# One transformer pass with mixture of experts on one core: expert FFN steps of 2048 and 1536 columns in place of 1024, weight loads in runs of 8 and 6 KB, and 64 token slots without branches where weights stay whole

## The chip, the cores and the metric

The kernel runs on one NeuronCore of a Trainium2 chip. TensorE (PE) multiplies, VectorE (DVE) and ScalarE (ACT) work on elements, GpSimd (POOL) does small things and issues some loads, and SyncE (SP) issues nearly all DMAs, which 16 DMA engines carry out. The metric is the device time of one execution in microseconds (us); lower is better. About 0.2% (2.7 us) is what a measurement of this kernel can tell from no change.

## The reference

256 tokens of width 1024, all in fp32, go through two blocks. The first is a latent attention (MLA) with a dense SwiGLU FFN, the second a sparse attention (NSA) with a mixture of experts; a scaled residual and a layer norm follow each part. What this change touches is the last part alone:

```python
logits = (xt @ w_router)                      # 256 x 8
top_val, top_idx = lax.top_k(logits, 2)       # each token goes to 2 of 8 experts
wts = softmax(top_val)
# for every expert e and the tokens that chose it:
h = silu(xb @ w_gate[e]) * (xb @ w_up[e])     # 1024 -> 3584
y[tok] += (h @ w_down[e]) * weight            # 3584 -> 1024
```

The 256 tokens make 512 assignments, 64 per expert on average. The weights of the eight experts are 8 x 3 x 1024 x 3584 x 4 bytes = 352.3 MB, of 431 MB that the kernel moves in all.

## The kernel before

**Places.** The experts are worked through one after the other, in eight "places". Place 0 is expert 0; `arrange()` sorts the others by their token counts and puts the three with most tokens at places 1, 3 and 5. At the places of `PLAIN = 0, 2, 4, 6, 7` the weights are used as they come, as fp32 matrices; at 1, 3 and 5 every weight tile is first split on ACT (`act.copy`, line 120, to tile `whi`) and DVE (`tensor_tensor`, line 123, to `wlo`), and a product takes three fp32r matmuls: x-high by w-high, x-high by w-low, x-low by w-high. Only place 0's first 512 columns are done differently, for all tokens at once, while the routing is still being worked out.

**Steps.** A place is cut along the 3584 FFN columns into the steps of `widths(e)`: 1024, 1024, 1024 and 512 columns (place 0: 512 first). A step reads its gate chunks (`mg`), then its up chunks (`mu`), then the down chunks (`md`) of the step before it, in that order on PE, and the loads are planned in the same order by `moe_keys()`. A chunk is one tile of 128 partitions x 2048 floats, 1 MB. Of gate and up a partition gets two rows' pieces of 1024 columns (4 KB each), or in the step of 512 columns four pieces of 2 KB; of down it gets two rows of 4 KB.

**Buffers.** Each chunk has its place in SBUF long before it is needed: the lists `first` and `then` go round 13 tiles of 1 MB (five `raw`, then `s1`, `xTh`, `xTl`, `xna`, `s2`, `x3Tl`, the pair `whi`/`wlo` in two halves with a DMA each, and, once place 0 is through, `x3Th`). The first 18 chunks are fetched while the attention still runs. After that SP issues a chunk's DMA (line 94, line 81 for the pair) when the tile's last reader is done: the matmuls at a plain place, DVE's subtraction at a split one.

**Branches.** The number of token slots depends on a count that is known only at run time. So PE has both versions of each group of matmuls and jumps (`big_or_small`): at plain places `two()` for at most 64 tokens, which puts 64 slots twice on the array's 128 columns, each half with half of the weight columns, and `one()` for up to 128 slots; at split places `three()` or, for at most 64 tokens, `two()`. So that later instructions may read a whole PSUM bank in both cases, `two()` at plain places also fills unused banks with a zero product (`blank`: the matmuls of line 1689 that read `low`, into `pa` and `pt`), and ACT copies half a bank to `low` for `whole()`. Line 1689 is the helper `mm`, which issues every expert matmul; tiles tell them apart: `pa` is gate or up, `pb` is down, `raw` (or `whi`, `wlo` as buffers) the weights at plain places, `whi`/`wlo` with 128*128 the split ones.

**Around a place.** `gather` picks the tokens by one-hot matmuls (line 1493), `hid` (1510, 1511) does silu and product from PSUM, the hidden tile is transposed on PE (1538, 1560) and copied out (1518, 1519, 1565), `outs` and `scatter` (442, 443, 1844 to 1846) add the result to `y`. At the end `end()` works off the last down chunks, scatters and normalizes. A path for more than 128 tokens stands behind the end (`vmax > 128`).

Of the kernel before, what the change touches and what calls it, by code (L numbers as in the profile page):

```python
# [20 lines left out]
E = 8  # L21
# [5 lines left out]
def body(tc, a, out, tap=None, upto=9):  # L27
# [39 lines left out]
    def load(src, shape, where=None):  # L67
# [9 lines left out]
        if isinstance(where, list):  # L77
            rs = [w()[:, :h] for w in where]
            m = shape[0] // 2
            for i in range(2):  # L80
                sp.dma_start(rs[i].rearrange("p (a b) -> p a b", a=m), src[:, i * m:(i + 1) * m, :])
            return rs, n, shape
        r = where()
        v = r[:, :n]
        v = v.rearrange("p (a b) -> p a b", a=shape[0])
# [72 lines left out]
    for z in ("s1", "s2", "x3Th", "x3Tl"):  # L158
        places[z] = lambda z=z: slot(ep, z)()
# [206 lines left out]

    def moe_shape(key):
        c0, wd = widths(key[1])[key[2]]
        return (2, 1024) if key[0] == "md" and not key[4:] or key[0] != "md" and wd == 1024 else (4, 512)

    def moe_src(key):
        k, e, j, i = key[:4]
        c0, wd = widths(e)[j]
        w = a[{"mg": "moe_w_gate", "mu": "moe_w_up", "md": "moe_w_down"}[k]][0]
        w = w[0] if e == 0 else w[bass.ds(order[e], 1)][0]
        if k == "md":
            if key[4:]:
# [1679 lines left out]
```

## Time and profile before

| what | value |
|---|---|
| median of 3 runs | 1371.7 us (1371.13 to 1372.74) |
| the profiled execution's own time | 1371.53 us |
| its span, first to last instruction | 1369.8 us |
| moved | 430.95 MB, 168,529 packets |
| PE / DVE / ACT busy | 1309.6 / 741.7 / 632.0 us |
| granted TensorE clock, mean | 0.991 |

The profile is of one execution. 1.7 us of its time lie outside the span. PE's busy time is the union of overlapping matmuls whose ends are modelled, so a full row of nines on PE does not say that PE is the bound. A share of the DMA engines above 1 comes from packets that overlap on one engine.

### The profile page before, as it was taken

To read this page: it belongs to the slowest core of one execution; us is meant where nothing else is said; L and a number is where in the kernel's file an instruction comes from. 1 tells how busy PE (TensorE), PEld (TensorE's weight loads), DVE (VectorE), ACT (ScalarE), POOL (GpSimd) and SP (SyncE) were. 2 spreads that over 40 slices of the span, in tenths; PEclk is the share of its full clock that TensorE was granted. 3 is DMA by queue.
4 is the path that set the end of the run, shared out by engine and by line. 5 is a ranking of instruction groups with operands and counts; after the bars stand their busy time and mean duration, and the time that the engine had idled before them with its cause. 6 is when DMAs were issued, how large, how long until landed. Compare 5 with 4: busy or idle time off the path is not lost. (4 is left out here: it accounts for less than half of the span.)

```text
span 1369.8 us, 20185 instructions
## 1 busy us (share of the span) xinstructions
PE 1309.6 (96%) x7310; PEld 918.5 (67%) x7310; DVE 741.7 (54%) x1213; ACT 632.0 (46%) x989; POOL 42.8 (3%) x58
## 2 busy tenths in 40 slices
PE   8998999999999899999999999999999999998885
PEld 7878999989988683368874467884446886442331
DVE  5856545577678851268872158883227986200103
ACT  5554444446576540258771057882027885010001
POOL 0002000002000110000000000000000000000000
PEclk9999999999999999999999999999999999999998
DMA  9634555579522659999999999999999999999994
GB/s 312 208 119 156 184 186 185 185 206 253 170 82 67 230 206 356 409 408 408 402 407 408 402 409 408 403 407 405 407 403 408 409 400 389 409 402 409 409 402 158
DMA packets 168529, 430.95 MB, mean 315 GB/s; under 512 B 11935, under 2 KB 64421, under 8 KB 168400
## 3 DMA queue, kind: packets, MB, share of 16 engines
q1 hardware_dynamic: 165824, 421.00, 81.6%
q0 software_dynamic: 2576, 8.18, 2.0%
q8 instruction: 87, 1.43, 0.4%
q14 instruction: 42, 0.34, 0.1%
HBM read 428.08 MB, written 1.07 MB: 313 GB/s over the span
## 5 line engine op out<-in xcount | busy, mean ns | idle before, releaser
L123 DVE TENSOR_TENSOR wlo<-raw,whi 128x1024 fp32r<-128x1024 f32 (+1 forms) x341 | 404.6, 1215 | 186.8 <-ACT whi L120 176.7
L120 ACT CAST whi<-raw 128x1024 fp32r<-128x1024 f32 (+2 forms) x343 | 353.9, 1045 | 196.1 <-PE pa L1689 41.0
L1689 PE MATMUL pa<-raw,xe 128*64 128x512 f32 (+1 forms) x1128 | 233.2, 554 | 8.3 <-DMA raw<-in_moe_w_up_dram 4.4
L1689 PE MATMUL pa<-whi,xe 128*128 128x512 f32 (+2 forms) x716 | 229.8, 407 | 1.7 <-ACT whi L120 1.5
L1689 PEld LDWEIGHTS pa<-raw,xe 128*64 128x64 f32 x1128 | 77.8, 137 | 142.4 <-issue 107.6
L1689 PEld LDWEIGHTS pa<-whi,xe 128*128 128x128 f32 (+1 forms) x716 | 130.4, 186 | 40.4 <-issue 5.2
L1689 PE MATMUL pa<-wlo,xe 128*128 128x512 f32 (+2 forms) x380 | 142.8, 411 | 1.3 <-DVE wlo L123 1.2
L1689 PE MATMUL pb<-raw,four 128*64 128x512 f32 x528 | 130.5, 597 | 11.5 <-DMA raw<-in_moe_w_down_dram 8.4
L1565 ACT COPY four<-pt 128x512 f32<-128x512 f32 x19 | 11.1, 585 | 231.6 <-PE pt L1560 200.5
L1689 PE MATMUL pb<-whi,four 128*128 128x512 f32 (+1 forms) x352 | 115.1, 404 | 0.0
L1689 PEld LDWEIGHTS pb<-raw,four 128*64 128x64 f32 x528 | 39.0, 136 | 87.5 <-issue 71.4
L1511 DVE TENSOR_TENSOR four<-four,pa 128x512 f32<-128x512 f32 x57 | 36.9, 683 | 106.2 <-PE pa L1689 78.0
L1565 DVE COPY four<-pt 128x512 f32<-128x512 f32 x15 | 10.4, 691 | 152.7 <-PE pt L1689 152.7
L1689 PEld LDWEIGHTS pa<-wlo,xe 128*128 128x128 f32 (+1 forms) x380 | 66.7, 183 | 20.8 <-issue 3.1
L1689 PEld LDWEIGHTS pb<-whi,four 128*128 128x128 f32 (+1 forms) x352 | 65.3, 186 | 15.0
L1689 PE MATMUL pb<-wlo,four 128*128 128x512 f32 (+1 forms) x184 | 73.8, 412 | 0.0
L261 PE MATMUL pa<-xTh,whi 128*128 128x256 f32 x216 | 67.6, 313 | 0.0
L263 PE MATMUL pa<-xTh,wlo 128*128 128x256 f32 x216 | 61.1, 283 | 0.4 <-DVE wlo L123 0.4
L262 PE MATMUL pa<-xTl,whi 128*128 128x256 f32 x216 | 61.1, 283 | 0.0
L261 PE MATMUL pb<-xTh,whi 128*128 128x256 f32 x176 | 49.9, 284 | 0.0
L262 PE MATMUL pb<-xTl,whi 128*128 128x256 f32 x176 | 49.8, 283 | 0.0
L263 PE MATMUL pb<-xTh,wlo 128*128 128x256 f32 x176 | 49.8, 283 | 0.0
(423 smaller groups left out, 2075.5 us busy)
## 6 DMA issues: line engine op xcount, KB each, us to landing
raw<-in_moe_w_up_dram SPq DMA_DIRECT2D x105, 1024.0 KB, 16.5
raw<-in_moe_w_down_dram SPq DMA_DIRECT2D x102, 1024.0 KB, 16.4
raw<-in_moe_w_gate_dram SPq DMA_DIRECT2D x99, 1024.0 KB, 17.5
raw<-in_nsa_w_in_dram SPq DMA_DIRECT2D x23, 512.0 KB, 7.1
raw<-in_ffn_w_gate_dram SPq DMA_DIRECT2D x11, 1024.0 KB, 5.1
raw<-in_ffn_w_up_dram SPq DMA_DIRECT2D x11, 1024.0 KB, 5.1
raw<-in_ffn_w_down_dram SPq DMA_DIRECT2D x11, 1024.0 KB, 4.8
wlo<-in_moe_w_gate_dram SPq DMA_DIRECT2D x11, 512.0 KB, 15.7
```

The lines of the kernel that those rows point to most:

```text
L120: act.copy(hi[:, :h], src)
L123: (pool if later == "pool" else dve).tensor_tensor(lo[:, :h], src, f(hi[:, :h]), op=ALU.subtract)
L261: pe.matmul(o, lh, rh, start=first, stop=False)
L262: pe.matmul(o, lh, rl, start=False, stop=False)
L263: pe.matmul(o, ll, rh, start=False, stop=last)
L1511: dve.tensor_tensor(hh, sg, pu, op=ALU.mult)
L1565: eng(hT[:, i * 512:(i + 1) * 512], p)
L1689: pe.matmul(o, l, r, start=first, stop=last, skip_group_check=True)
```

## The change

1. **Wider steps, longer runs.** Steps are 2048 and 1536 columns (place 0: 512, 2048, 1024). A gate or up chunk of a wide step is 128 rows x the whole step: one run of 8 KB per partition (1 MB), or of 6 KB (768 KB). A down chunk gives a partition two neighbouring rows, one run of 8 KB, instead of rows p and p + 128; for this the hidden columns are taken odd and even (`hh[:, o:o + 255:2]`, `z[:, q::2]`) when they are transposed or multiplied. The last two down tails stay at 2 KB, and so does place 0's first step.
2. **64 slots, no branches.** Plain places always take 64 slots: two matmuls side by side, one with the even and one with the odd weight columns, read with a stride of two floats. Split places always take three passes. `big_or_small`, `blank`, `low`, `whole`, `fold`, `upper`, `count0` and the masks go. A place with more tokens than its slots (64 or 128) is finished by a generic path behind the end, which is entered if `over > 0`.
3. **Order.** A step is now gate, first half of the earlier step's down chunks, up, second half; loads are planned in that order. Silu runs right after gate, from four PSUM banks to one tile `hh` (one buffer, in the room of `s1`), so one tile fewer takes chunks. `arrange` and the gather of the next place move with the steps.

```diff
-    def widths(e):
-
-        if e == 0:
-            return [(0, 512), (512, 1024), (1536, 1024), (2560, 1024)]
-        return [(0, 1024), (1024, 1024), (2048, 1024), (3072, 512)]
+    def widths(e, gen=False):
+        if e == 0 and not gen:
+            return [(0, 512), (512, 2048), (2560, 1024)]
+        return [(0, 2048), (2048, 1536)]
...
+    def step_of(key):
+        return widths(key[1], key[4:] == ("gen",))[key[2]]
     def moe_shape(key):
-        c0, wd = widths(key[1])[key[2]]
-        return (2, 1024) if key[0] == "md" and not key[4:] or key[0] != "md" and wd == 1024 else (4, 512)
+        wd = step_of(key)[1]
+        if key[0] == "md":
+            return (4, 512) if key[4:] == ("tail",) else (2, 1024)
+        return (4, 512) if wd == 512 else (2, 1024) if wd == 1024 else (2, wd // 2)
+    def n_gu(wd):
+        return 8 if wd > 1024 else wd // 256
     def moe_src(key):
         k, e, j, i = key[:4]
-        c0, wd = widths(e)[j]
+        c0, wd = step_of(key)
         w = a[{"mg": "moe_w_gate", "mu": "moe_w_up", "md": "moe_w_down"}[k]][0]
         w = w[0] if e == 0 else w[bass.ds(order[e], 1)][0]
+        if key[4:] == ("tail",):
+            r0 = c0 + wd - 512
+            return [w[r:r + 256, i * 512:(i + 1) * 512].rearrange("(p k) n -> p k n", k=2) for r in (r0, r0 + 256)]
         if k == "md":
-            if key[4:]:
-                return w[c0:c0 + 512, i * 512:(i + 1) * 512].rearrange("(k p) n -> p k n", p=128)
             r0 = c0 + i * 256
-            return w[r0:r0 + 256, :].rearrange("(k p) n -> p k n", p=128)
-        m = 2 if wd == 1024 else 4
-        return w.rearrange("(k p) n -> p k n", p=128)[:, m * i:m * i + m, c0:c0 + wd]
+            return w[r0:r0 + 256, :].rearrange("(p k) n -> p (k n)", k=2)
+        if wd <= 1024:
+            m = 8 // n_gu(wd)
+            return w.rearrange("(k p) n -> p k n", p=128)[:, m * i:m * i + m, c0:c0 + wd]
+        return w[i * 128:i * 128 + 128, c0:c0 + wd]
     def moe_keys():
         prev = None
         for e in range(E):
             for j, (c0, wd) in enumerate(widths(e)):
-                for k in ("mg", "mu"):
-                    yield from ((k, e, j, i) for i in range(wd // 256))
-                if prev:
-                    m = widths(prev[0])[prev[1]][1] // 256
-                    yield from (("md", *prev, i) for i in ((0, 2, 1, 3) if m == 4 and prev[0] in PLAIN else range(m)))
+                m = widths(prev[0])[prev[1]][1] // 256 if prev else 0
+                for k, ds in (("mg", range((m + 1) // 2)), ("mu", range((m + 1) // 2, m))):
+                    yield from ((k, e, j, i) for i in range(n_gu(wd)))
+                    yield from (("md", *prev, i) for i in ds)
                 prev = e, j
-        yield from (("md", *prev, i, 1) for i in range(2))
-
-    first = [["four"] * 2] * 4 + ["raw"] * 5 + ["s1", "xe", "xTh", "xTl", "xna", "xe", "s2", "x3Tl", ["whi", "wlo"]]
-    then = ["raw"] * 5 + ["s1", "xTh", "xTl", "xna", "s2", "x3Tl", ["whi", "wlo"]]
...
+        yield from (("md", *prev, i) for i in range(wd // 256 - 2))
+        yield from (("md", *prev, i, "tail") for i in range(2))
+    first = [["four"] * 2] * 4 + ["hh"] + ["raw"] * 5 + ["xe", "xTh", "xTl", "xna", "xe", "s2", "x3Tl", ["whi", "wlo"]]
+    then = ["raw"] * 5 + ["xTh", "xTl", "xna", "s2", "x3Tl", ["whi", "wlo"]]
     keys = list(moe_keys())
-    seq = first + then * 4 + (then + ["x3Th"]) * 30
+    seq = first + then * 2 + (then + ["x3Th"]) * 30
...
-            slot_of = iota[:, base:base + 128]
-            if base == 0:
-                slot_of = ep.tile([128, 128], F32, tag="slot", bufs=1, name=nm("slot"))
-                dve.scalar_tensor_tensor(slot_of, upper, fold[:, e:e + 1], iota[:, :128], op0=ALU.mult, op1=ALU.add)
+            slot_of = twice if G["plain"] else iota[:, base:base + 128]
...
             p = S["p"]
+            m = 64 if G["plain"] else 128
             for i in range(i0, i0 + 2):
                 k = 4 * kk + i
                 for t in range(2):
-                    pe.matmul(p[:, i * 128:(i + 1) * 128], x3[:, t, k * 128:(k + 1) * 128], f(G["oh"][:, t, :]),
+                    pe.matmul(p[:, i * m:i * m + m], x3[:, t, k * 128:(k + 1) * 128], f(G["oh"][:, t, :m]),
...
+    def hid_T(hh, wd, plain):
+        hT, ths = [], []
+        def go(c0, n):
+            p = pT()
+            for c in range(c0, c0 + n):
+                o = c // 2 * 256 + c % 2
+                pe.transpose(p[:, (c - c0) * 128:(c - c0 + 1) * 128],
+                             hh[:, c * 128:c * 128 + 128] if plain else hh[:, o:o + 255:2], ident)
+            if plain:
+                if c0 == 0:
+                    hT.append(four())
+                z = hT[0][:, c0 * 128:(c0 + n) * 128]
+                (dve.tensor_copy if c0 else act.copy)(z, p[:, :n * 128])
+                hT.extend(hT[0][:, c * 128:c * 128 + 128] for c in range(c0, c0 + n))
+                if c0 + n == m:
+                    del hT[0]
+            else:
+                z = four(F32R).rearrange("p (c n) -> p c n", c=4)
+                pv = p.rearrange("p (c n) -> p c n", c=4)
+                act.copy(z[:, :, :128], pv)
+                dve.tensor_tensor(z[:, :, 128:], pv, f(z[:, :, :128]), op=ALU.subtract)
+                hT.extend(z[:, c] for c in range(4))
+        m = wd // 256 if plain else wd // 128
+        return hT, [lambda c=c: go(c, min(4, m - c)) for c in range(0, m, 4)]
...
-
-
-    count0 = nc.values_load_multi_w_load_instructions(cnti[0:1, 0:1], engines=[mybir.EngineType.PE], min_val=0,
-                                                      max_val=256)[1][0]
-
-
-    def is_big(n):
-        return n[0] > 64 if n[1] is None else (n[0] & n[1]) < 1
...
-
-    def passes(n, todo, post=None):
-
-
-        def three():
-            for o, x, (rh, rl), first, last in todo:
-                mm(o, x[:, 0:128], rh, first, False)
-                mm(o, x[:, 0:128], rl, False, False)
-                mm(o, x[:, 128:256], rh, False, last)
...
+    def gate_up(which, e, j, G, gen):
+        wd, x = widths(e, gen)[j][1], G["xe"]
+        nc_ = n_gu(wd)
+        if G["plain"]:
+            bw = min(512, wd // 2) if nc_ < 8 else wd // 4
+            b = [pA()[:, :bw] for _ in range(wd // 2 // bw)]
+            for i in range(nc_):
+                key = which, e, j, i
+                for r, z in enumerate(raw_of(*key)):
+                    k, o = (i, b[r]) if nc_ == 8 else (2 * i + r, b[0])
+                    for q in range(2):
+                        mm(o[64 * q:64 * q + 64], x[:, k, 0:64], z[:, q::2], k == 0, k == 7)
                 used(*key)
+                rest()
+                fill(2)
+            return b
+        assert nc_ == 8
+        bw = wd // 4
+        b = [pA()[:, :bw] for _ in range(4)]
+        for i in range(8):
+            w = wmoe(which, e, j, i, *gen)
+            for r in range(2):
+                hi, lo = w(r)
+                for h in range(2):
+                    o, c = b[2 * r + h], slice(h * bw, h * bw + bw)
+                    mm(o, x[:, i, 0:128], hi[:, c], i == 0, False)
+                    mm(o, x[:, i, 0:128], lo[:, c], False, False)
+                    mm(o, x[:, i, 128:256], hi[:, c], False, i == 7)
             rest()
             fill(2)
         return b
+    def hidden_tile():
+        return ep.tile([128, 2048], F32, tag="hh", bufs=1, name=nm("hh"))
+    def each_bank(hh, b):
+        o = 0
+        for p in b:
+            yield hh[:, o:o + p.shape[-1]], p
+            o += p.shape[-1]
+    def down(at, which):
+        e, j, G, hT, acc, gen = at
+        ss = widths(e, gen)
+        for i in which:
+            first, last = j == i == 0, j == len(ss) - 1 and i == ss[j][1] // 256 - 1
+            if G["plain"]:
+                key = "md", e, j, i
+                z = raw_of(*key)
+                for hf in range(2):
                     for q in range(2):
+                        mm(acc[hf][64 * q:64 * q + 64], hT[i][:, 64 * q:64 * q + 64], z[q][:, H[hf]], first, last)
+                used(*key)
+            else:
+                w = wmoe("md", e, j, i, *gen)
+                for kk in range(2):
+                    hi, lo = w(kk)
+                    x = hT[2 * i + kk]
+                    for hf in range(2):
+                        mm(acc[hf], x[:, 0:128], hi[:, H[hf]], first and kk == 0, False)
+                        mm(acc[hf], x[:, 0:128], lo[:, H[hf]], False, False)
+                        mm(acc[hf], x[:, 128:256], hi[:, H[hf]], False, last and kk == 1)
             rest()
+            fill(1)
...
+                last_j = j == len(ss) - 1
+                final = last_j and n == len(todo) - 1
+                if last_j and not final:
                     nxt, th = gather(*todo[n + 1])
                     th[0]()
+                g = gate_up("mg", e, j, G, gen)
+                fill(99)
+                if len(order) == 1:
+                    arrange()
+                hh = hidden_tile()
+                for z, p in each_bank(hh, g):
+                    act.activation(z, p, AF.Silu)
+                m = 0
+                if at is not None:
+                    if at[1] == 0:
+                        acc = [pB(), pB()]
+                    at = (*at[:4], acc, gen)
+                    m = widths(at[0], gen)[at[1]][1] // 256
+                    down(at, range((m + 1) // 2))
+                if last_j and not final:
+                    fq.extend(th[1:])
+                u = gate_up("mu", e, j, G, gen)
+                fill(99)
+                for z, p in each_bank(hh, u):
+                    dve.tensor_tensor(z, z, p, op=ALU.mult)
+                hT, ths = hid_T(hh, wd, G["plain"])
+                if final:
+                    now(ths[:0])
+                    down(at, range((m + 1) // 2, (m + 1) // 2 + 1))
+                    now(ths)
+                    down(at, range((m + 1) // 2 + 1, m))
+                else:
+                    down(at, range((m + 1) // 2, m)) if at is not None else None
+                    if at is not None and at[0] != e:
+                        scatters(at)
+                    fq.extend(ths)
+                at = (e, j, G, hT)
...
+    assert not halves and not fq and all(c.uses == [0, 0] for c in plan)
     man.close()
     free.clear()
     free.extend(z for z in range(HL) if z not in given)
-    vmax = nc.values_load(cnti[0:1, 1:2], min_val=0, max_val=256)
-    with tc.If(vmax > 128):
+    over = nc.values_load(ordi[0:1, 16:17], min_val=0, max_val=256)
+    with tc.If(over > 0):
         for e in range(E):
-            with tc.If(nc.values_load(ordi[0:1, e:e + 1], min_val=0, max_val=256) > 128):
-                G, th = gather(e, 128)
-                now(th)
-                run([(e, 128)], G, None)
+            count = nc.values_load(ordi[0:1, e:e + 1], min_val=0, max_val=256)
+            for base in (64, 192) if e in PLAIN else (128,):
+                with tc.If(count > base):
+                    G, th = gather(e, base, True)
+                    now(th)
+                    run([(e, base)], G, None, ("gen",))
         scr, z = norm_tiles()
```

## Rows read from the trace of the kernel before

**Rows 1.** The page, share of the 16 DMA engines and GB/s in 40 slices.

```profile
DMA  9634555579522659999999999999999999999994
GB/s 312 208 119 156 184 186 185 185 206 253 170 82 67 230 206 356 409 408 408 402 407 408 402 409 408 403 407 405 407 403 408 409 400 389 409 402 409 409 402 158
```

**Rows 2.** Windows: stretch, its length, busy us of each engine, clock, DMA share, GB/s.

```profile
900.00:910.00 10.00, 10.00 (x45) 8.11 (x44) 9.58 (x10) 8.81 (x11) 0.00 (x0) 1.00 1.02 408
887.00:897.00 10.00, 10.00 (x54) 8.41 (x54) 5.21 (x6) 6.90 (x10) 0.00 (x0) 1.00 1.05 394
1244.00:1320.00 76.00, 63.68 (x263) 20.63 (x261) 9.44 (x14) 6.00 (x11) 0.00 (x0) 1.00 1.03 408
```

**Rows 3.** DMA packets of 887 to 897, then of 900 to 910.

```profile
DMA packets 1633, 3.94 MB, mean 394 GB/s; under 512 B 59, under 2 KB 59, under 8 KB 1631
...
DMA packets 1066, 4.08 MB, mean 408 GB/s; under 512 B 72, under 2 KB 72, under 8 KB 1065
```

**Rows 4.** Windows of whole places: place 5 (split), place 6 (plain), columns as before.

```profile
1021.17:1151.10 129.93, 126.49 (x565) 100.44 (x565) 107.86 (x104) 101.64 (x115) 0.00 (x0) 0.99 1.03 405
1151.10:1240.00 88.90, 88.53 (x450) 38.04 (x451) 16.79 (x24) 11.24 (x19) 0.00 (x0) 1.00 1.02 401
```

**Rows 5.** Line 1689's forms: duration ns min/median/max, first and last start us.

```profile
L1689 PE MATMUL pa<-raw,xe x1128: 379/592/644, 516.0 to 1335.6; 128*64 128x512 f32 x152, 128*64 128x256 f32 x36
...
L1689 PE MATMUL pa<-wlo,xe x380: 379/393/643, 540.4 to 1254.5; 128*128 128x512 f32 x168, 128*64 128x512 f32 x14, 128*64 128x256 f32 x8
...
L1689 PE MATMUL pa<-low x38: 384/498/505, 523.0 to 1335.9; 128*128 128x512 f32 x30, 128*128 128x256 f32 x8
...
L1689 PE MATMUL pt<-low x19: 355/481/481, 542.0 to 1342.9; 128*128 128x512 f32 x15, 128*128 128x256 f32 x4
```

**Rows 6.** Loads to `raw`, issue to landing, in 1020:1050, 1120:1160 and 1244:1320.

```profile
DMA to landing us min/median/max: 16.9/17.8/20.3
...
DMA to landing us min/median/max: 9.3/12.5/14.7
...
DMA to landing us min/median/max: 14.6/18.1/20.4
```

**Rows 7.** Timeline of PE: dense FFN, split place, plain place.

```profile
262.02 0.28 PE L263 MATMUL pt<-xTh,wlo 128*128 128x256 f32 x1
...
265.98 0.28 PE L263 MATMUL pt<-xTh,wlo 128*128 128x256 f32 x1
...
680.63 0.40 PE L1689 MATMUL pb<-wlo,four 128*128 128x512 f32 x1
...
687.61 0.40 PE L1689 MATMUL pb<-wlo,four 128*128 128x512 f32 x1
...
722.02 7.09 PE L1689 MATMUL pa<-raw,xe 128*64 128x512 f32 x32
729.04 0.50 PE L1689 MATMUL pa<-low 128*128 128x512 f32 x1
729.38 0.39 PE L1689 MATMUL pb<-whi,four 128*128 128x512 f32 x1
...
1008.71 3.67 PE L1689 MATMUL pa<-raw,xe 128*64 128x256 f32 x32
```

**Rows 8.** Timeline: start of the plain work, start of place 1, end.

```profile
509.77 3.73 PE L1493 MATMUL pt<-oh,x 128*128 128x128 f32 x32
...
511.42 0.69 DVE L443 TENSOR_TENSOR four<-four,four 128x512 fp32r<-128x512 f32 x1 [0.68 <-ACT four L442]
...
513.26 1.99 PE L1579 MATMUL pt<-oh,four 128*128 128x128 f32 x16
...
518.33 7.43 SPq L94 DMA_DIRECT2D raw<-in_moe_w_up_dram  x4
...
583.45 0.50 PE L1689 MATMUL pa<-whi,xe 128*128 128x512 f32 x1
...
1349.69 0.58 ACT L442 CAST four<-pb 128x512 fp32r<-128x512 f32 x1 [5.79 <-PE pb L1689]
```

More of the change, by code (lines that the diff above doesn't have):

```diff
@@ L157, in body @@
         places[z] = slot(xp, z)
-    for z in ("s1", "s2", "x3Th", "x3Tl"):
+    for z in ("hh", "s2", "x3Th", "x3Tl"):
         places[z] = lambda z=z: slot(ep, z)()
@@ L1464, in dense, with gather @@
             mm3(p, sl(x3T, slice(None), kk, slice(t * 128, t * 128 + 128)), w(k), kk == 0, kk == 7)
-    def gather(e, base):
-        G = {"n": None, "plain": e in PLAIN and base == 0}
+    def gather(e, base, gen=False):
+        G = {"plain": e in PLAIN and not gen}
         def onehot():
@@ L1832, in down_tail @@
+    def down_tail(at, i):
+        e, j, G, hT, acc, gen = at
+        key = "md", e, j, i, "tail"
+        w = raw_of(*key)
+        for m in range(2):
+            for q in range(2):
+                mm(acc[i][64 * q:64 * q + 64], hT[m - 2][:, 64 * q:64 * q + 64], w[2 * m + q], False, m == 1)
             fill(2)
-        done_with(key)
+        used(*key)
     def outs(acc, hf):
@@ L1847, in scatter, with run @@
                                  accum_out=sums[t][:, hf:hf + 1] if sums is not None else None)
-    def hidden_of(b, u, G, e):
-        hs = [hid(g, z) for g, z in zip(b, u)]
-        return lambda: hid_T_plain(hs, G["n"]) if G["plain"] else hid_T(hs, G["n"])
-    def run(todo, G, prev, end=None):
-        pend = None
-        small = []
+    def run(todo, G, at, gen=(), end=None):
+        nxt, acc = None, None
         for n, (e, base) in enumerate(todo):
-            nxt = None
-            for j in range(4):
-                if prev is not None and prev[:2] == (e, j):
+            ss = widths(e, gen)
+            for j, (c0, wd) in enumerate(ss):
+                if at is not None and at[:2] == (e, j):
@@ L1862, in run @@
                     continue
-                last = n == len(todo) - 1 and j == 3
-                if G["plain"]:
-                    g = ffn_plain("mg", e, j, G)
-                else:
-                    g = ffn("mg", e, j, G)
-                if prev is not None:
-                    phT = prev[3]()
-                if j == 1 and len(order) == 1:
-                    arrange()
-                if j == 1 and n > 0:
-                    fq.extend([lambda hf=hf, t=t, a=pend: scatter(*a, hf, t) for hf in range(2) for t in range(2)])
@@ L1918, in run, with scatters @@
             return
-        down(e, 3, hT, acc, G)
-        for hf in range(2):
-            oo.append(outs(acc, hf))
-        for hf in range(2):
-            for t in range(2):
-                scatter(e, oo, G["ohT"], hf, t)
+        down(at, range(m))
+        scatters(at)
+        fill(99)
+    def scatters(at):
+        e, _, G, _, acc, _ = at
+        oo = [outs(acc, hf) for hf in range(2)]
+        fq.extend([lambda hf=hf, t=t: scatter(e, oo, G["ohT"], hf, t) for hf in range(2) for t in range(2)])
@@ L1967, in end @@
         norm_rest(z)
-    G0["n"] = count0, None
-    run([(e, 0) for e in range(E)], G0, (0, 0, G0, lambda: hT0), end)
+    run([(e, 0) for e in range(E)], G0, (0, 0, G0, hT0), (), end)
     auto[0] = False
-    assert not halves and all(c.uses == [0, 0] for c in plan)
+    assert not halves and not fq and all(c.uses == [0, 0] for c in plan)
     man.close()
@@ L2018, in constants @@
     c["turn"] = np.tile(np.array([0.0, 1, 7, 2, 6, 3, 5, 4]), (128, 1))
-    c["power"] = np.tile(2.0 ** e, (128, 1))
+    c["most"] = np.tile(np.where(np.isin(e, PLAIN), 64.0, 128.0), (128, 1))
     packed = np.concatenate([c[k].astype(np.float32) for k, _ in CONST_COLS], 1)
```

271 lines of the change are left out of this document (34 added, 237 removed).

## The prediction

> **What bounds the kernel.** I read the slices of the whole span first. From about 515 us to 1345 us the DMA engines are full and move about 408 GB/s [rows 1]; before that they wait for the attention. This stretch is 60% of the span and does nothing but the experts. PE shows nines there too, so both could be the bound, and the next views separate them.
>
> The windows by place: at a split place (three passes) PE is busy 126.5 of 129.9 us, at the plain place behind it 88.5 of 88.9 us [rows 4]. A place is 44.04 MB, which at 408 GB/s takes 108 us. So PE is slower than the loads at a split place and faster at a plain one, and the chunk buffers carry the difference. The landing times show how far: around 1020 to 1050, where a split place begins, a load is 17.8 us in flight, seven chunks queued and nothing in stock; at 1120 to 1160, where it ends, the shortest is 9.3 us, since landed chunks sit in the tiles [rows 6]. The rate hardly drops. After 1240 two plain places in a row have used the stock up: PE is busy 63.7 of 76 us, the DMA still gives 408 GB/s [rows 2]. Over the stretch the DMA sets the time, PE follows closely, and the last down chunk is the last thing waited for: ACT takes the first finished half at 1349.7 us, and 20.1 us of scatter and norm follow [rows 8]. DVE, at 107.9 us, and ACT, at 101.6 us of a split place [rows 4], are nowhere ahead of PE.
>
> **What a packet costs.** A window in which the 2 KB runs of the 512-column step arrive has 394 GB/s, one with 4 KB runs 408 [rows 2]. Their packets [rows 3], without the small ones: 1574 for 3.94 MB and 994 for 4.08 MB, each in 10 us of 16 engines, that is 160 us of engine time. With o per packet and b per MB, 160 = 1574 o + 3.94 b and 160 = 994 o + 4.08 b give o = 8.9 ns, b = 37.0 us per MB. Rounding of the MB leaves o between 8 and 10. A 1.049 MB chunk then takes (256 x 0.0089 + 38.8) / 16 = 2.57 us at 4 KB, which is the 408 GB/s seen; 2.71 at 2 KB; and 2.50 us at 8 KB, if one run stays one packet. A 0.786 MB chunk in 6 KB runs takes 1.89 us.
>
> **The change, part by part.**
>
> *Runs.* A place now has 38 chunks of 256 packets and 4 of 512, 11,776 in all; after the change 46 chunks of 128, plus some 490 because about one chunk in twelve lands in `whi`/`wlo` with its runs halved: 6,380. The difference, 5,400 x 8.9 ns / 16 = 3.0 us per place. Seven places give -21.0 us; place 0 has 13 down chunks still to come, -0.9 us. Runs of 8 KB from this queue do not occur in the trace. From below: if only the 2 KB step's loss goes, 4 x 0.14 = 0.6 us per place, -4 us. From above: o = 10 ns, -24.7 us. I take the middle figure, since 2 and 4 KB lie on one line and only a cut of the run would leave it.
>
> [...] The trace has 8.9 ns between 2 and 4 KB, so I hold to the trace.
>
> *First refill.* The first chunk at place 0 now lies in `hh`, which takes no new load, so the first tile that comes free is the second chunk's. The four chunks of the old gate step take PE about 7.0 us [rows 7], so that is 1.7 us later than the 518.3 at which SP now issues the first load [rows 8]. The DMA has little queued then [rows 1]: +1.7 us.
>
> *Narrower gather.* The plain one-hots cover 64 slots: half of 3.73 and 1.99 us on PE [rows 8]. But line 1579 also needs DVE's split of the hidden tile, done at 512.1, so only part shows: I take -1.2 us (bounds 0 and -2.9). The PE load of `count0` goes with it.
>
> *Gate and up at plain places.* The same records as before, 64 columns by 512 or 384. Today 32 of them take 7.02 us, 0.22 us each (two run side by side), and 256 wide at most 0.115 [rows 7]. 384 lies between: no change. Gate and up from `raw` have no form but 128*64, and w-low is multiplied in 128*128, but for the few chunks that lie in `wlo` as a buffer [rows 5]: plain places have at most 64 tokens, split places more, and nothing follows the norm. So the counts fit the new slots and the generic path stays shut. The 57 zero products go [rows 5], 0.34 us each at 512 columns [rows 7], about 3.6 us per place: PE needs some 84.9 us there. [...] I take nothing.
>
> *Split places.* Steps of 1536 use four banks of 384 columns where 512 would need three. Dense matmuls of 256 take 0.120 us (33 in 3.96), of 512 0.233 [rows 7], so 384 about 0.176: 192 x 0.176 = 33.8 against 144 x 0.233 = 33.6 us. Nothing. PE stays near 126 us.
>
> *Longer steps.* At a split step all four banks are taken by gate and again by up, so up waits for four silus, the next gate for four products, each 0.6 to 0.7 us. Half of the earlier step's down chunks stands in between, at least two chunks, 3.5 us: hidden, except that DVE's next splits queue behind 2.7 us of products. I take nothing on the total because PE has stock there; without it, some 2 us for each of six split steps.
>
> *One buffer fewer.* Twelve tiles of 1 MB. Plain work starts at 516.0 [rows 5] and place 1 at 583.4 [rows 8], 67 us, 65 without zero products. So PE without waits would end place 5 at 516 + 65 + 3 x 126 + 2 x 84.9 = 1129 us. The last load now lands at about 1349, just ahead of ACT's copy [rows 8]; 21 us earlier that is 1328, and two places of 108.5 - 3.0 = 105.5 us before it the loads have place 5 in, at about 1117. They are 12 us ahead, five chunks, and in flight they need about four [rows 6]: nine or ten of twelve. Hidden, with some 8 us to spare.
>
> *Sum.* -21.0 - 0.9 + 1.7 - 1.2 = -21.4 us from 1371.5 us, the profiled execution's own time (its span is 1369.8); the median is 1371.7. Forecast **1350 us**.
>
> **Rivals.**
>
> *The stride slows PE* (ends slower). For x us more per plain place, 3x - 8 us is lost by the end of place 5, as the tiles fill; the last two places hide 20 us each. Gate and up of a plain place take 24 x 8 records of 0.22 us and 4 x 16 of 0.11 [rows 7], 49 us. From x = 10, a fifth of that, it is slower than before; at half as much again, x = 24, 64 + 2 x 4 us are lost: 1422 us; at twice, 139 + 57: 1546. For it: PE and the loads are level over a split and a plain place, 211 us each. [...]
>
> *Long runs save less than counted.* The 8.9 ns were seen between 2 and 4 KB; part of it may be a trait of the short runs. If half of it holds, 5,400 x 4.45 / 16 = 1.5 us per place are saved, 1361 us in the end. If runs are cut at 4 KB, -4 + 0.5: 1368 us. For it: no load here has a longer run. Against: 2.57 us from the fit gives the 408 GB/s of a stretch that is not in it [rows 2]. [...]
>
> *PE's waits at the longer steps take the gain.* If each split place costs PE 10 us more, 30 us against 8 spare: 22 lost, 1372 us; at half, 7 lost, 1357. For it: one tile for `hh`, all banks in use. Against: down chunks between.
>
> **Chances.** As forecast, 1343 to 1357 us: 0.60. Long runs saving less, 1358 to 1369: 0.13. Waits at steps, 1357 to 1372: 0.11. Stride or another PE loss, slower: 0.14. Better than 1343: 0.02. Faster by over 0.2% (about what a measurement tells): 0.79, within 0.2%: 0.06 out of the second and third, slower: 0.15. The range, 1343 to 1372 us, holds all but the slower side and the best case; its lower end is o = 10 ns with the whole gather gain.
>
> **What would show it.** Right: about 420 GB/s at the experts, plain records still 0.22 us, a mean of a split window near 126 us of PE, the last down chunk landing near 1328, about 20 us behind it. Wrong on the packet: 408 GB/s with 4 KB packets, or 412 with 8 KB. Wrong on the stride: 32 records of gate in clearly over 7 us, and DMA slices under 400. Wrong on buffers: landing times under 9 us and a dip in GB/s at the end of places 1, 3 and 5.

## The result, and the profile after

The changed kernel takes **1349.13 us** (median of 4 runs, 1348.41 to 1351.52) against 1371.41 before, run beside it: the ratio is 0.984, 95% interval 0.9823 to 0.9857, or 22.3 us less. The profiled execution took 1349.32 us, its span 1347.5. The forecast was 1350. The mean granted clock is 0.991 in both.

The page of the kernel after, share of the DMA engines, GB/s and packets, answers to [rows 1]:

```profile
DMA  9635555569622477999999999999999999999994
GB/s 315 211 107 177 165 181 187 188 193 278 197 66 78 146 276 270 410 418 418 417 419 415 418 419 419 416 420 399 418 420 419 416 419 400 418 417 420 418 419 172
DMA packets 127944, 430.56 MB, mean 320 GB/s; under 512 B 12463, under 2 KB 64949, under 8 KB 99808
```

Nearly the same bytes in 40,600 packets fewer than before; the slices of the experts rose from about 406 to about 418. Two of them, 399 and 400, stand out, and the windows (columns as in [rows 2]) show why:

```profile
516.00:1237.00 721.00, 721.00 (x3528) 453.81 (x3524) 374.27 (x399) 316.37 (x380) 0.00 (x0) 1.00 1.01 413
900.00:910.00 10.00, 10.00 (x45) 8.02 (x44) 9.43 (x11) 5.73 (x6) 0.00 (x0) 1.00 1.02 417
910.00:920.00 10.00, 10.00 (x48) 4.52 (x48) 2.94 (x4) 3.60 (x6) 0.00 (x0) 1.00 0.99 383
1130.00:1140.00 10.00, 10.00 (x47) 3.28 (x48) 5.32 (x5) 4.37 (x5) 0.00 (x0) 1.00 0.99 367
1004.04:1124.30 120.26, 120.26 (x596) 98.67 (x594) 93.93 (x97) 80.61 (x94) 0.00 (x0) 1.00 1.02 418
1244.00:1320.00 76.00, 63.35 (x296) 19.98 (x292) 7.80 (x12) 3.33 (x6) 0.00 (x0) 1.00 1.02 418
```

The loads dip where the split places 3 and 5 end (383, 367), and from 516 to 1237 PE is not idle for a moment; only in the last two places does it wait for loads, as before (63.4 of 76 us). The split window is shorter than that of [rows 4], but the two don't compare: its last step is longer now, and more of its down chunks come after it. From one split place to the next does compare. The timeline of PE after: the first plain gates, the start of places 3 and 5 (split) and of place 6 (plain):

```profile
515.73 14.62 PE L1631 MATMUL pa<-raw,xe 128*64 128x512 f32 x64
...
531.90 7.37 PE L1631 MATMUL pa<-raw,xe 128*64 128x512 f32 x32
...
791.33 0.50 PE L1631 MATMUL pa<-whi,xe 128*128 128x512 f32 x1
...
1004.05 0.50 PE L1631 MATMUL pa<-whi,xe 128*128 128x512 f32 x1
...
1124.27 1.12 PE L1631 MATMUL pa<-whi,xe 128*64 128x512 f32 x4
```

A split and a plain place take 1004.05 - 791.33 = 212.7 us; before, by the same view, 1021.17 - 802.64 = 218.5:

```profile
802.64 0.49 PE L1689 MATMUL pa<-whi,xe 128*128 128x512 f32 x1
...
1021.17 0.49 PE L1689 MATMUL pa<-whi,xe 128*128 128x512 f32 x1 [1.46 <-ACT whi L120]
```

32 strided records of 512 columns take 7.37 us where 32 took 7.09 [rows 7]. (A record is one matmul in the trace.)

The DMA view after, packets of 900 to 910, and the loads issued from 1110 to 1140 and from 1244 to 1320 (median us to landing last):

```profile
DMA packets 716, 4.17 MB, mean 417 GB/s; under 512 B 80, under 2 KB 80, under 8 KB 336
...
raw<-in_moe_w_up_dram SPq DMA_DIRECT2D x7, 1024.0 KB, 7.3
...
raw<-in_moe_w_down_dram SPq DMA_DIRECT2D x13, 1024.0 KB, 16.5
```

The fit of the prediction, made on 2 and 4 KB runs [rows 3], holds at 8 KB: without the small ones 636 x 8.9 ns + 4.17 x 37.0 us = 160.0 us, which are 10 us of 16 engines. At the end of place 5 a load lands after 7.3 us, under the 9.3 seen before [rows 6]: the queue is short because SP has no tile to fill (from 1110 to 1140 it waits 12.7 us for PE and 10.7 us for DVE to give tiles back).

Start and end of the expert stretch after, answering to [rows 8]:

```profile
509.99 3.68 PE L1500 MATMUL pt<-oh,x 128*128 128x64 f32 x32
513.48 2.05 PE L1557 MATMUL pt<-oh,four 128*128 128x64 f32 x16
...
519.59 3.93 SPq L91 DMA_DIRECT2D raw<-in_moe_w_up_dram  x3
...
1326.39 0.59 ACT L462 CAST four<-pb 128x512 fp32r<-128x512 f32 x1 [17.97 <-PE pb L1631]
```

The end, 1326.39 in place of 1349.69, is 23.3 us earlier. The gathers are as long as before.

### The profile page after: what moved, and what is told of

Its sections match the earlier page's. It is cut to its first block, busy times and chain, and to the rows that moved or that the text cites. A ratio compares the mean times of both kernels' runs of the same rounds, so it can differ in the third digit from the quotient of the medians.

```text
span 1347.5 us, 19685 instructions
## 1 busy us (share of the span) xinstructions
PE 1300.5 (97%) x7397; PEld 925.1 (69%) x7397; DVE 729.6 (54%) x1208; ACT 597.3 (44%) x949; POOL 42.3 (3%) x57
## 2 busy tenths in 40 slices
DMA packets 127944, 430.56 MB, mean 320 GB/s; under 512 B 12463, under 2 KB 64949, under 8 KB 99808
## 5 line engine op out<-in xcount | busy, mean ns | idle before, releaser
L131 DVE TENSOR_TENSOR wlo<-raw,whi 128x1024 fp32r<-128x1024 f32 (+2 forms) x365 | 413.7, 1152 | 225.2 <-ACT whi L128 216.2
L128 ACT CAST whi<-raw 128x1024 fp32r<-128x1024 f32 (+3 forms) x367 | 360.0, 994 | 255.2 <-PE pa L1631 63.7
L1631 PE MATMUL pa<-raw,xe 128*64 128x512 f32 (+1 forms) x1112 | 238.8, 570 | 6.2 <-DMA raw<-in_moe_w_up_dram 6.2
L1631 PE MATMUL pa<-whi,xe 128*128 128x512 f32 (+3 forms) x820 | 240.2, 382 | 0.0
L1631 PEld LDWEIGHTS pa<-whi,xe 128*128 128x128 f32 (+1 forms) x820 | 145.9, 185 | 30.5 <-issue 8.3
L1631 PE MATMUL pa<-wlo,xe 128*128 128x512 f32 (+3 forms) x436 | 153.2, 389 | 0.0
L1631 PE MATMUL pb<-raw,four 128*64 128x512 f32 x520 | 119.0, 596 | 8.4 <-DMA raw<-in_moe_w_down_dram 8.4
L1763 DVE TENSOR_TENSOR hh<-hh,pa 128x512 f32<-128x512 f32 (+1 forms) x43 | 25.0, 620 | 145.1 <-PE pa L1631 144.9
L1631 PEld LDWEIGHTS pa<-wlo,xe 128*128 128x128 f32 (+1 forms) x436 | 75.9, 182 | 15.2 <-issue 5.2
L1750 ACT ACTIVATE hh<-pa 128x512 f32<-128x512 f32 (+1 forms) x43 | 21.5, 547 | 73.8 <-PE pa L1631 73.8
```

What stands on the lines that cost most here:

```text
L128: act.copy(hi[:, :h], src)
L131: (pool if later == "pool" else dve).tensor_tensor(lo[:, :h], src, f(hi[:, :h]), op=ALU.subtract)
L1631: pe.matmul(o, l, r, start=first, stop=last, skip_group_check=True)
L1750: act.activation(z, p, AF.Silu)
L1763: dve.tensor_tensor(z, z, p, op=ALU.mult)
```

## The experiments

Theory T: the gain is the loads' cost per packet, and the rest lies behind the loads. Theory P: the gain is PE's, freed of branches, zero products and short steps.

**Runs halved again, all, or one kind alone.** Steps, chunk sizes and products stay; only the shape of a chunk changes:

```diff
-        return w[i * 128:i * 128 + 128, c0:c0 + wd]
+        h = wd // 2
+        return w.rearrange("(k p) n -> p k n", p=128)[:, i // 2 * 2:i // 2 * 2 + 2, c0 + i % 2 * h:c0 + i % 2 * h + h]
...
-            return w[r0:r0 + 256, :].rearrange("(p k) n -> p (k n)", k=2)
+            return w[r0:r0 + 256, :].rearrange("(k p) n -> p k n", p=128)
...
-                        mm(o[64 * q:64 * q + 64], x[:, k, 0:64], z[:, q::2], k == 0, k == 7)
+                        zq = z.rearrange("p (c q n) -> p q c n", q=2, n=128)[:, q]
+                        mm(o[64 * q:64 * q + 64].rearrange("p (c n) -> p c n", n=128), x[:, k, 0:64], zq, k == 0, k == 7)
...
```

The transposes and the banks follow the new order of columns.

> The kernel after the change, but every chunk in runs half as long: gate and up chunks are two row blocks by half of the step's columns (4 KB and 3 KB), down chunks two blocks of 128 rows (4 KB), so that the odd and even columns become neighbouring blocks of 128 and the stride of two goes as well. Steps, tiles, chunk sizes and PE's products are those after the change. Theory T (the gain is the loads' cost per packet; all else lies behind the loads): 46 chunks of a place have 128 packets more, less some 490 that were halved anyway, 5,400 x 8.9 ns / 16 = 3.0 us for each of seven places and about 1 us for place 0, +22 us, of which up to 3 come back because slower loads leave PE more slack at the ends of the split places: 1368 to 1371 us, GB/s at the experts back to about 408. Theory P (the gain comes from PE, which was freed of branches on counts, zero products and short steps): all of that stays, 1347 to 1351 us.

> Only gate and up in halved runs (4 KB and 3 KB); down chunks stay at 8 KB and the stride of two stays. Theory T: 32 chunks of a place with 128 packets more, less a twelfth, 3,750 x 8.9 ns / 16 = 2.1 us for seven places and under 1 us at place 0, 15 us less up to 3 of slack: 1361 to 1365 us. Theory P: 1348 to 1351 us.

> Only the down chunks in halved runs (4 KB), with the odd and even columns as neighbouring blocks of 128, so without the stride; gate and up stay at 8 KB and 6 KB. Theory T: 14 chunks of a place (12 of the last), less a twelfth, 1,640 x 8.9 ns / 16 = 0.9 us for seven places, +6.4 us, less up to 3 of slack: 1353 to 1356 us; with the run before it this adds up to the one with all runs halved. Theory P: 1347 to 1350 us, since PE has lost the stride.

Measured medians, with the packets of each page:

| kernel | us | packets |
|---|---|---|
| all halved | 1369.53 (1366.87 to 1370.48, 10 runs) | 169,031 |
| gate and up halved | 1363.18 (1362.14 to 1364.24) | 155,976 |
| down halved, no stride | 1353.56 (1352.42 to 1355.58) | 141,000 |
| after | 1349.13 | 127,944 |
| before | 1371.41, 1372.02 beside these | 168,529 |

All three fall where T put them, and P, as the whole cause, is out. With every run halved the ratio to before is 0.998 (0.997 to 0.999): some 2.5 us, and no more, remain of the change without its long runs. The page of that kernel is the one of before again in its GB/s, and PE waits at the start of places 3 and 5, 217.6 us apart:

```profile
GB/s 316 201 109 171 175 177 188 185 201 275 170 78 63 213 207 331 409 409 405 405 409 406 405 409 406 404 409 408 404 408 409 403 408 404 404 406 409 406 405 177
```

```profile
795.32 0.50 PE L1632 MATMUL pa<-whi,xe 128*128 128x512 f32 x1 [1.57 <-ACT whi L128]
...
1012.89 0.50 PE L1632 MATMUL pa<-whi,xe 128*128 128x512 f32 x1 [1.76 <-ACT whi L128]
```

**One long run in the kernel before.** The other way round: only the down chunks of before as single runs.

```diff
...
-            return w[r0:r0 + 256, :].rearrange("(k p) n -> p k n", p=128)
+            return w[r0:r0 + 256, :].rearrange("(p k) n -> p (k n)", k=2)
```

> The kernel before the change with one thing of it: each down chunk of 256 rows is loaded so that a partition takes two neighbouring rows, one run of 8 KB in place of two of 4 KB. The hidden columns aren't reordered, so they meet other rows of the down matrix and the output is another one; PE's work, its branches and the steps of 1024 columns stay. Theory T: 14 chunks of a place (12 of the last, 13 still to load at place 0), less a twelfth that lands in halves, 102 x 128 x 8.9 ns / 16 = 7.3 us less: 1364 to 1365 us. Theory P: 1371 to 1372 us, since nothing of PE changes.

1365.31 us (1364.28 to 1366.05), ratio 0.9953 (0.9936 to 0.997): 6.4 us of the 7.3, with PE's work as it was. T stands again.

**The stride alone.** The transposes take neighbouring columns too.

```diff
...
-                        mm(o[64 * q:64 * q + 64], x[:, k, 0:64], z[:, q::2], k == 0, k == 7)
+                        zq = z.rearrange("p (c q n) -> p q c n", q=2, n=128)[:, q]
+                        mm(o[64 * q:64 * q + 64].rearrange("p (c n) -> p c n", n=128), x[:, k, 0:64], zq, k == 0, k == 7)
```

> The kernel after the change, but gate and up of the plain places read two neighbouring blocks of 128 columns where they read odd and even ones, and the transposes likewise; the down chunks stay at 8 KB, so that hidden columns meet other rows of the down matrix than they should: the work is the same, the values aren't. Measures the stride alone. The strided records run at 0.226 us where those before ran at 0.219, 1.5 to 2 us of PE for each plain place. Theory T: this lies behind the loads but for the dips at the ends of the split places, 1.5 us each at two of them: records back at 0.219 us, the dips gone or smaller, 1346 to 1349 us. Rival S (the stride holds PE up on the path): 4 plain places and place 0 give back 2 us each or more, 1340 us or less.

1347.86 us (1346.08 to 1348.75), 1.3 less than after; the intervals of the two ratios (0.9808 to 0.9841 here) overlap, so the time alone settles little. The trace does more. PE's timeline after the change (64 records at place 4), then PE's timeline and the windows of this kernel:

```profile
936.89 14.62 PE L1631 MATMUL pa<-raw,xe 128*64 128x512 f32 x64
```

```profile
516.59 15.13 PE L1631 MATMUL pa<-raw,xe 128*64 128x512 f32 x64
...
533.26 7.03 PE L1631 MATMUL pa<-raw,xe 128*64 128x512 f32 x32
...
788.57 0.50 PE L1631 MATMUL pa<-whi,xe 128*128 128x512 f32 x1
...
933.90 13.95 PE L1631 MATMUL pa<-raw,xe 128*64 128x512 f32 x64
...
999.37 0.50 PE L1631 MATMUL pa<-whi,xe 128*128 128x512 f32 x1
```

```profile
910.00:920.00 10.00, 10.00 (x52) 3.83 (x50) 5.44 (x7) 5.44 (x7) 0.00 (x0) 1.00 1.01 412
1130.00:1140.00 10.00, 10.00 (x47) 4.64 (x44) 3.08 (x4) 3.25 (x5) 0.00 (x0) 1.00 1.01 413
```

32 records take 7.03 us where the strided ones take 7.37, and 64 take 13.95 where they take 14.62: 5% more with the stride. Only the first 64 of this kernel are slower, 15.13 us: the granted clock was 0.54 from 516.5 to 519.2 in this execution, and 0.46 x 2.7 = 1.2 us are about what lies between 15.13 and the 13.95 of place 4. After the change it was 1.00 there, so place 0 doesn't compare. Two places take 210.8 us where they took 212.7, and the dips are nearly gone: 5 us at 384 GB/s from 1125 on are left. A stride of two costs 1.9 us per plain place (more, if the loads now set these 210.8). In the time 1.3 us of it show, less than a measurement can tell.

**Less work for PE, less work for the loads.** The first leaves out the product of x-low and w-high at split places, the second multiplies every even down chunk twice in place of loading the odd one.

```diff
-                    mm(o, x[:, i, 0:128], lo[:, c], False, False)
-                    mm(o, x[:, i, 128:256], hi[:, c], False, i == 7)
+                    mm(o, x[:, i, 0:128], lo[:, c], False, i == 7)
...
```

Down goes the same way.

> The kernel after the change without one of the three products of a split place (the low part of x with the high part of w, in gate, up and down), which makes the output less exact and takes a third of PE's work from three places: 126 us each become about 84. Theory T (the loads set the end): only the two dips of the GB/s at the ends of the split places go, 1.5 us each: 1345 to 1348 us, and PE has gaps in the split places. Theory P (PE at the split places sets the time): 3 x 42 us of PE go, and with the loads as the next bound the end comes well ahead of that: under 1335 us.

```diff
-                    yield from (("md", *prev, i) for i in ds)
+                    yield from (("md", *prev, i) for i in ds if i % 2 == 0)
...
-                key = "md", e, j, i
+                key = "md", e, j, i // 2 * 2
...
```

> The kernel after the change with every second down chunk left out of the loads: the chunk before it is multiplied in its place, so that PE's work stays and 7 of a place's 44 MB aren't loaded (the output is another one). Measures how far PE is behind the loads. A chunk of 8 KB runs takes 2.49 us, so the loads of a place take 105.4 - 17.4 = 88 us. Theory T: PE becomes the bound. Plain work starts at 515.7 us, place 0 takes 65, three split places 126 each, four plain ones 85 to 88 each, and the norm 20: 1319 to 1331 us, so the gain of the loads can't grow by more than 20 to 30 us before PE ends it. Theory P (PE sets the time as it is): 1347 to 1350 us. If loads alone mattered it would be 1349 - 7.5 x 17.4 = 1219 us.

With a third of PE's work gone from three places: 1348.03 us (1346.55 to 1348.29), 1.1 less. With a sixth of the bytes gone: 1331.13 us (1329.79 to 1332.13), 18.0 less, and no more. So the loads by themselves end near 1348, PE by itself at 1331. Window 516 to 1237 and the start of places 3 and 5, first with PE's third gone, then with the bytes gone:

```profile
516.00:1237.00 721.00, 661.99 (x2982) 358.21 (x2983) 361.82 (x399) 303.81 (x381) 0.00 (x0) 0.96 1.01 415
```

```profile
785.98 0.50 PE L1631 MATMUL pa<-whi,xe 128*128 128x512 f32 x1 [1.67 <-ACT whi L128]
...
997.85 0.49 PE L1631 MATMUL pa<-whi,xe 128*128 128x512 f32 x1 [1.67 <-ACT whi L128]
```

```profile
516.00:1237.00 721.00, 721.00 (x3526) 455.07 (x3526) 326.30 (x357) 274.29 (x339) 0.00 (x0) 1.00 0.89 351
```

```profile
792.83 0.50 PE L1631 MATMUL pa<-whi,xe 128*128 128x512 f32 x1
...
1005.33 0.50 PE L1631 MATMUL pa<-whi,xe 128*128 128x512 f32 x1
...
1125.52 2.02 PE L1631 MATMUL pa<-raw,xe 128*64 128x512 f32 x8
```

Two places take the loads 211.9 us (first pair) and PE 212.5 us (second); after the change they take 212.7. It is a dead heat up to the end of place 5, and PE's 18 us are all gained in the last two places: with the bytes gone place 6 begins at 1125.52, and after the change it began at 1124.27. SP's waits from 905 to 940 say the same: after the change it waits for PE and DVE to give tiles back,

```profile
SPq L91 <- PE pa L1631: 19.2, 9, 4.6
SPq L91 <- DVE wlo L131: 8.3, 3, 3.6
```

and with PE's third gone for earlier loads to land:

```profile
SPq L91 <- DMA raw<-in_moe_w_up_dram: 11.7, 6, 2.0
SPq L91 <- DMA raw<-in_moe_w_down_dram: 4.4, 3, 2.0
```

**More work for PE at plain places.** The first products of gate and up are repeated, each time starting the sum anew.

```diff
-                        mm(o[64 * q:64 * q + 64], x[:, k, 0:64], z[:, q::2], k == 0, k == 7)
+                        for _ in range(4 if k == 0 else 1):
+                            mm(o[64 * q:64 * q + 64], x[:, k, 0:64], z[:, q::2], k == 0, k == 7)
```

> The kernel after the change, where at the plain places the first row block of each gate and up bank is multiplied four times in place of once (each time it starts the sum anew, so the result stays). Per plain place 24 records of 512 columns more at 0.226 us and 24 of 384 at about 0.17: x = 9.5 us of PE. It puts a number to the ledger of the prediction's rival on the stride, a loss of 3x - 8 us by the end of place 5 with both last places hiding theirs: 349 + 1000 + 20 = 1370 us. Theory T': the dips at the ends of places 3 and 5 show that the spare is used up, and the loss is nearer to 3x: 1374 to 1378 us. If PE had room at the plain places: 1349 us.

1452.86 us (1451.72 to 1454.17), 104 more: far outside every figure. The first cause is my count: a product is two records, so 96 came on per plain place, not 48, 19 us at 0.226 and 0.17. The second is their order, four copies of one column half behind each other: a first chunk took 9.41 us for 32 records where it had taken 2.02 for 8, so 0.31 us for each record more. PE's timeline: that chunk at place 4, after the change and here; then places 3, 5 and 6 here:

```profile
911.62 2.02 PE L1631 MATMUL pa<-raw,xe 128*64 128x512 f32 x8
```

```profile
958.37 9.41 PE L1631 MATMUL pa<-raw,xe 128*64 128x512 f32 x32
```

```profile
838.07 0.50 PE L1631 MATMUL pa<-whi,xe 128*128 128x512 f32 x1
...
1076.86 0.51 PE L1631 MATMUL pa<-whi,xe 128*128 128x512 f32 x1
...
1197.08 3.44 PE L1631 MATMUL pa<-whi,xe 128*64 128x512 f32 x10
```

Two places take 238.8 us, so x was 26.1 us. At that size the ledger of the prediction's stride rival gives 3 x 26.1 - 8 = 70 us by the end of place 5, and 2 x (26.1 - 20) = 12 after it, 82 us. Place 6 begins 1197.08 - 1124.27 = 72.8 us later; the last two places cost some 30 more, not 12. The first part comes close only because place 0 has fewer of these products: place 1 begins 20.6 us later, so 20.6 + 2 x 26.1 = 72.8 us were added by the end of place 5, with PE busy throughout, and none of them was hidden. So both parts of the ledger fail, the second one more. Two smaller doses, with the halves side by side and only one bank (four times is shown; twice has 2 for 4):

```diff
-                    for q in range(2):
-                        mm(o[64 * q:64 * q + 64], x[:, k, 0:64], z[:, q::2], k == 0, k == 7)
+                    for n in range(4 if k == 0 and o is b[0] else 1):
+                        for q in range(2):
+                            mm(o[64 * q:64 * q + 64], x[:, k, 0:64], z[:, q::2], k == 0, k == 7)
```

> The kernel after the change, where at the plain places the first product of the first bank of each gate and up, both column halves side by side, is made four times in place of once (each starts the sum anew, so the result stays). A product is two records; 12 more of each gate at 0.226 us, or 0.17 at 384 columns: x = 2 x 2.7 + 2 x 2.0 = 9.5 us per plain place. The run with 122 us more of PE work showed 104 of them in the time; the one with half of the down loads left out showed PE at 1331 us, 18 ahead of the loads. The prediction's ledger for extra PE work (3x - 8, both last places hiding theirs): 1349 + 20 = 1369 us. Theory T' (no spare at the ends of the split places, the last two places hide theirs): 3x = 28, 1374 to 1378 us. Theory T'' (what shows is all of the extra work, 5x, less 18): 1379 us.

> As the run with x = 9.5 us, but the product is made twice in place of four times: x = 3.2 us per plain place, about what the zero products of before took there (3.6). It tells whether PE's shortening was needed for the gain of the longer runs. The ledger 3x - 8: 1350 to 1351 us. Theory T' (no spare, 3x): 1357 to 1359 us. Theory T'' (5x less 18): 1349 us.

Four times: 1388.20 us (1384.89 to 1388.91), 39.1 more. Twice: 1360.72 (1359.83 to 1361.83), 11.6 more. T' comes nearest to the second (1357 to 1359); none is near the first. Place 6 begins, with the product twice and then four times:

```profile
1134.48 2.02 PE L1631 MATMUL pa<-whi,xe 128*64 128x512 f32 x8
```

```profile
1156.56 2.92 PE L1631 MATMUL pa<-whi,xe 128*64 128x512 f32 x12
```

With 3.2 us at places 2 and 4 and 3.6 at place 0, PE had 10.0 us more to do; place 6 begins 10.2 us later and the kernel ends 11.6 later. So PE has no spare up to there. With 9.5, place 6 begins 32.3 us later, against 29.8 worked out (in this execution the plain work began 1.2 us later, and the granted clock was 0.53 in its first 2.8 us, 0.83 from 510 to 520), and the last two places add 6.8 of their 19. They hid 12 us here and 21 in the large dose, both together, and not 20 each.

The small dose says one thing more. It is about the time of the zero products that the change took away (3.2 of 3.6 us per plain place, though at another spot), and with it only 11 of the 22 us are left: half of what the long runs bring needed PE to get shorter in the same change.

**The order of the first chunks.**

```diff
-    first = [["four"] * 2] * 4 + ["hh"] + ["raw"] * 5 + ["xe", ...
+    first = [["four"] * 2] * 4 + ["raw"] * 5 + ["hh"] + ["xe", ...
```

> The kernel after the change, but the chunk that lies in hh at the start is the sixth of its gate step and not the first, so that the first chunk multiplied lies in a raw tile and gives it back at once. Theory T (the first refill comes one chunk late, the prediction's +1.7 us): the first load is issued one chunk, 14.5 / 8 = 1.8 us, before 519.6 us, and the end moves with it by 1.0 to 1.8 us: 1347.3 to 1348.1 us. Rival: the DMA has enough queued at this point, or PE's lack of spare at the ends of the split places takes it back: 1348.8 to 1349.5 us.

1349.32 us (1348.50 to 1351.32), the rival's figure. A gain of 1.0 to 1.8 us is less than a time can tell here, but the traces agree with none: place 6 begins at 1124.01 in place of 1124.27, and the span is 1347.5 us in both. SP does issue earlier, but the third row of the windows 510 to 540 shows the loads pause ten us later instead (after, the three rows had 212, 345 and 394):

```profile
517.56 3.93 SPq L91 DMA_DIRECT2D raw<-in_moe_w_up_dram  x3
```

```profile
510.00:520.00 10.00, 10.00 (x69) 6.79 (x70) 3.99 (x13) 2.02 (x5) 0.00 (x0) 1.00 0.70 249
520.00:530.00 10.00, 10.00 (x48) 3.15 (x46) 0.00 (x0) 0.60 (x1) 0.00 (x0) 1.00 1.00 394
530.00:540.00 10.00, 10.00 (x48) 3.24 (x46) 0.00 (x0) 0.60 (x1) 0.00 (x0) 1.00 0.94 345
```

**The gather.**

```diff
-                    pe.matmul(p[:, i * m:i * m + m], x3[:, t, k * 128:(k + 1) * 128], f(G["oh"][:, t, :m]),
+                    pe.matmul(p[:, i * 128:i * 128 + 128], x3[:, t, k * 128:(k + 1) * 128], f(G["oh"][:, t, :128]),
...
```

> The kernel after the change, but the gathers of the plain places (tokens, and the hidden columns of the first step) multiply with 128 columns of the one-hot again in place of 64; what is taken from the result stays 64 wide. The prediction took 1.2 us for the narrower gather. Theory T (the gather's records are as long with 64 columns as with 128, since 32 of either take 3.5 us): no change, 1348.8 to 1349.6 us. If the prediction's term holds: 1350.3 us.

1350.04 us (1349.56 to 1350.49), between the two figures, but its ratio, 0.984 (0.9827 to 0.9853), is that of after. PE's timeline decides: 514.24 - 510.75 = 3.49 us with 128 columns, 513.48 - 509.99 = 3.49 with 64.

```profile
510.75 3.73 PE L1500 MATMUL pt<-oh,x 128*128 128x128 f32 x32
514.24 2.10 PE L1557 MATMUL pt<-oh,four 128*128 128x128 f32 x16
```

None of the kernels that do the whole computation is faster than the changed one.

## Why the prediction was right, and where not

**The runs (-21.9 us): right.** Halving them again costs 20.4 us, and 21.7 against the kernel without the stride, where the dips are nearly gone. The packets of 900 to 910 follow the fit, GB/s rose to 418 as said (about 420), and each kind of chunk brings its share in either kernel. Whether the cost lies in the packet or in the shorter run in memory, no run tells: here a run is a packet. And half of the gain rests on a condition that has no term in the sum, PE's shortening: with 3.2 us per plain place put back, 11 of 22 us are left.

The 41,000 packets more of the kernel with all runs halved (169,031 against 127,944) cost 20.4 us in the end, or 7.9 ns each on 16 engines.

**First refill (+1.7): 0 in the end.** SP's first load came 1.3 us later than before, but undoing it moved neither place 6 nor the span in the trace.

**Narrower gather (-1.2): 0.** The step that failed is "half of 3.73 and 1.99 us". 109 ns per record is not set by the columns streamed, since 64 and 128 take the same; the plain work began at 515.73, against 516.0 before [rows 5]. What sets it was not tried; the weights loaded for each record are 128x128 in both, by the trace. The two small terms, +1.7 and -1.2, were both wrong and nearly cancelled.

**The stride ("I take nothing"): 5% on the records**, at least 1.9 us per plain place, far from the rival's 10. That it costs nothing was the author's estimate, and no run shows it: 32 records with a stride of two floats take 7.37 us where 32 without it take 7.03, almost, not wholly, free.

**Longer steps, four banks of 384: 0, right.** Two places take PE 212.5 us; 126 + 84.9 + 1.9 for the stride is 212.8.

**One buffer fewer ("some 8 us to spare"): wrong.** By the sign that the prediction named, short landing times and a dip at the end of split places (here 3 and 5, not 1), the tiles are used up. Without the stride the dips are nearly gone; with it 3 x 1.9 = 5.7 us were asked by place 5 and about 1.3 lost (a difference within what a measurement can tell), so the spare was roughly 4 us rather than 8, and the stride used it. The rival's price for more PE work, 3x - 8 with 20 us hidden at each of the last two places, was therefore too low: x = 3.2 us cost 11.6, not 1.6. No run gave the lost tile back, so how much of this one tile more would have saved stays open.

So the sum was right because its one large term was right, and the +0.5 of the two small ones by luck. How close the next bound stood it had nearly right, 211 us each for PE and the loads under its stride rival; 212.5 and 211.9 were measured. What it had too large was the spare between them. Loads that were faster still would have gained only in the last two places: with a sixth of the bytes gone place 6 begins no earlier, and the 18 us come behind that. The 2.5 us (1372.02 - 1369.53) by which the kernel with halved runs and no stride beats the one before belong to the rest of the change (predicted +0.5); which part of it brings them was not separated.

## What to carry to other kernels

Where loads set the end, fit time = packets x o + bytes x b from two windows with different run lengths: it forecast a run length that the trace did not contain (about 420 GB/s, 418 measured). Before counting such a gain in full, work out the next engine's time over one whole period of the schedule (here a split and a plain place together), since buffers only shift work within it; a spare worked out from a few tiles is the weakest number. And a price per instruction should come from the gap between starts at two sizes, before a narrower one is called cheaper (here 3.49 us for 32 of 64 columns and of 128).

## Not expected

- One cost per packet, 8.9 ns, fits the loads from 2 up to 8 KB: 418 GB/s at 8 and 6 KB against 406 at half of that, on the same bytes. Counted by the end of the kernel, 7.9 ns of it show.
- An fp32 product of 128 x 64 by 512 is two records (8 for the four of a first chunk at place 4). Where the two column halves alternate, a record takes 0.226 us, and where four products of one half follow each other 0.31: the dose planned at 9.5 us of PE, 19 by the right count, was 26.1.
- SP issued its first load 2.0 us earlier (517.56 for 519.59), and the end did not move: the loads paused ten us later instead.
- The change without its long runs gains 2.5 us, and with them but with some 3 us of PE per plain place put back 11 us; both together make 22.
